# A hybrid attention/mLSTM layer on one core: low parts of the normalised input on GpSimd, their products one place later, two low parts of the weights ahead of sums, wider dummy products

## The chip, the core and the metric

The kernel runs on one NeuronCore of a Trainium2 chip. The metric is the device time of the program in microseconds (us), the median of several executions. Before the change it is 353.72 us (three runs, 353.4 to 353.92).

## The reference, cut to what matters

One layer, 256 tokens of width 1024, fp32. Only the first lines bear on this change:

```
ada = c @ w_ada + b_ada                                   # c: one row of 1024
shift, scale, gate = split(ada, 3)
h = rmsnorm(x, norm_w) * (1 + scale) + shift              # [256, 1024]
qa, ka, va, za, qm, km, vm, zm, om, ig, fg, ga, gm = split(h @ w_in)   # w_in: [1024, 11272]
...  # attention over qa, ka, va; a chunked mLSTM over qm, km, vm; two projections; gates
y = sigmoid(ga) * ya + sigmoid(gm) * ym
return x + gate * (y @ w_out)
```

## The kernel before

**Split products.** An fp32 matrix product is made of three passes of a faster type (fp32r). Each operand is written as a high part (the value rounded to fp32r) and a low part (the value less the high part), and high x high, high x low and low x high are added up in PSUM. For each piece of weights ScalarE makes the high part (`wrh`, later `wh`) by a cast, VectorE the low part (`wrl`, later `wl`) by a subtraction of two tiles. The normalised input gets the same: `hTh` and `hTl`, [128, 8, 256], with the 1024 rows of h in eight slices of 128.

**The norm phase** is the first 52 us. The eight slices k = 0..7 are worked off one after the other while their data stream in. For each, `adat` (two pieces of 512 KB: the columns of w_ada for scale and shift of that slice) and 128 rows of w_in (the first 1784 columns and the eight gate columns) are loaded on SyncE's queue in the order A0 W0 A1 W1 and so on. The sums over `adat` times c give the slice's scale `Ab` and shift `Bb`, ScalarE applies these to the transposed x, and TensorE adds the slice's products to four accumulators: `pm0`, `pm1`, `pm2` (512 columns each, two token halves) and `pg` (256). No scheduler is at work: each engine runs its instructions in the order in which they are written, and that order is the string `P1_STEPS`. A step is a letter and a slice number:

- `c`, `k`: VectorE's sums for scale and shift over `adat` (L152); `C` both for slice 0 (L145). `a`, `b`: ScalarE makes `Ab` (L156) and `Bb` (L160) of them
- `i`, `j`: ScalarE writes `hTh` (L166) and the unrounded `hf` (L170); `G`: the low part `hTl` = hf - hTh (L173); `H`: i and j of slice 0
- `w`, `x`, `y`: ScalarE's high parts of the weights, columns 0 to 512, 512 to 1024, 1024 to 1792 (L178). `U`, `z`, `v`: VectorE's low parts of the same three (L183)
- `P`, `Q`, `q`, `N`, `M`, `n`, `m`, `e`: products on TensorE (L194). A pair (ch, i) is accumulator ch and pass i, and one such pair is two matmuls, one for each token half. For accumulator 0 pass 1 is high x low of the weights and pass 2 the one with `hTl`; for the others pass 1 is the one with `hTl` and pass 2 that with the low weights
- `K`: dummy products on the identity, so that TensorE does not lie idle; `D`, `E`: transposes of x by a product with `diag`, for the first and second token half; `t`: copies of them; `R`: GpSimd fills a small table (L279, L284); `L`: next loads

Ahead of the steps stand `keep_clock(WARM)`, then four products `pc` that spread c over all partitions, ScalarE's copies of them to `cb` (the second operand of all sums), the sum of squares of x for the first token half on VectorE and for the second on ScalarE (L239), two small GpSimd steps that make `rsx` of each (L213, L214), and ScalarE's two `diag` tiles (L242), which scale the identity by rsx.

In the main phase after it (from 51.6 us) chunks of weights are split and multiplied in the same manner, without a step that the change touches.

Of the kernel before, what the change touches and what calls it, by code (L numbers as in the profile page):

```python
# [9 lines left out]
F32 = mybir.dt.float32  # L10
F32R = mybir.dt.float32r
AF = mybir.ActivationFunctionType
OP = mybir.AluOpType
# [25 lines left out]

P1_STEPS = ("K5 D0 D1 D2 E0 E1 E2 C0 w0 R0 R1 R2 R3 U0 H0 G0 t0 B0 P0 x0 z0 y0 t2 B1 t1 L1 c1 a1 w1 k1 v0 Q0 q0 n0 T3 m0 "
            + "".join(f"b{k} i{k} U{k} j{k} G{k} x{k} " + ("t3 " if k == 2 else "") + f"L2 c{k + 1} z{k} y{k} a{k + 1} "
                      f"w{k + 1} k{k + 1} v{k} e{k} " for k in range(1, 7))
            + "b7 i7 U7 j7 G7 x7 z7 y7 v7 P7 Q7 q7 N7 M7").split()
WARM = 5

KX = 248
NR = 1536 + KX + 8
# [15 lines left out]
def tile_hybrid(ctx: ExitStack, tc: tile.TileContext, x, c, params, params2, w_row, ada_mod, ada_gate,  # L65
                w_in, w_att_proj, w_ml_proj, w_out, out):
    nc = tc.nc
# [15 lines left out]
    ident = consts.tile([128, 128], F32, name="ident")  # L83
# [5 lines left out]
    hTh = consts.tile([128, KT, S], F32R, name="hTh")  # L89
    hTl = consts.tile([128, KT, S], F32R, name="hTl")  # L90
# [36 lines left out]
    adat, wrow, wsp, hf = {}, {}, {}, {}  # L127
# [21 lines left out]
    def modulation_sum(k, s):  # L149
        if s:  # L150
            sums[k] = ph.tile([128, 2], F32, name="sums", bufs=2)
        nc.vector.tensor_tensor_reduce(sq, adat[k][:, s], cb, 1.0, 0.0, OP.mult, OP.add, sums[k][:, s:s + 1])  # L152
# [9 lines left out]
    def modulate(k, parts="ij"):  # L162
        kc = slice(k, k + 1)
        src = xnT[:, k] if k else xps[0][:, 0]
        if "i" in parts:
            nc.scalar.activation(hTh[:, k], src, AF.Identity, scale=Ab[:, kc], bias=Bb[:, kc])  # L166
        if "j" not in parts:
            return
        hf[k] = ph.tile([128, S], F32, name="hf", bufs=2)
        nc.scalar.activation(hf[k], src, AF.Identity, scale=Ab[:, kc], bias=Bb[:, kc])  # L170

    def modulate_low(k):
        nc.vector.tensor_tensor(hTl[:, k], hf[k], hTh[:, k].bitcast(F32), op=OP.subtract)  # L173

    def split_hi(k, c0, c1, copy=nc.scalar.copy):
        if k not in wsp:
            wsp[k] = (ph.tile([128, NR], F32R, name="wrh", bufs=3), ph.tile([128, NR], F32R, name="wrl", bufs=3))
        copy(wsp[k][0][:, c0:c1], wrow[k][:, c0:c1])  # L178

    def split_low(k, e, c0, c1):  # L180
        h, l = wsp[k]
        cs = slice(c0, c1)
        e.tensor_tensor(l[:, cs], wrow[k][:, cs], h[:, cs].bitcast(F32), op=OP.subtract)  # L183

    def mm_row(k, ch, passes=(0, 1, 2)):
        h, l = wsp[k]
        n = 512 if ch < 3 else NR - 1536
        cs = slice(ch * 512, ch * 512 + n)
        ops = ((hTh, h), (hTl, h), (hTh, l)) if ch else ((hTh, h), (hTh, l), (hTl, h))
        for i in passes:  # L190
            a, b = ops[i]
            for t in range(2):

                nc.tensor.matmul(pm[ch][:, t], a[:, k, t * 128:(t + 1) * 128], b[:, cs],  # L194
                                 start=k == 0 and i == 0 and (ch < 3 or t == 0),
                                 stop=k == KT - 1 and i == 2 and (ch < 3 or t == 1), skip_group_check=ch == 3)
# [4 lines left out]
    def next_loads(n):  # L201
        while n and lp[0] < len(P1_LOADS):
            (load_ada if P1_LOADS[lp[0]][0] == "A" else load_row)(int(P1_LOADS[lp[0]][1]))
            lp[0] += 1
            n -= 1
# [15 lines left out]
    pw = pp.tile([128, 2, 512], F32, name="warm", tag="pm0")  # L221

    def keep_clock(n):
        for _ in range(n):
            nc.tensor.matmul(pw[:, 0, 0:128], ident, ident, start=True, stop=True)

    keep_clock(WARM)


    pc = [pp.tile([128, 512], F32, name="pc0", tag="pg"), pp.tile([128, D], F32, name="pc1", tag="pm2")]  # L230
    for j in range(4):
        n, q = divmod(j, 2)
        nc.tensor.matmul(pc[n][:, q * 256:(q + 1) * 256], pick[:, j:j + 1].to_broadcast([128, 128]), cparts,
                         start=q == 0, stop=q == 1, skip_group_check=True)
# [12 lines left out]
    def x_transposes(kp, ts=(0, 1)):  # L247
        if 0 in ts:
            xps[kp] = pp.tile([128, 2, 256], F32, name="xps", tag=("pm1", "aux1", "pg", "aux1")[kp])
        pa = xps[kp]  # L250
        for t in ts:
            for kk in range(2):
                k = 2 * kp + kk
                o, v = pa[:, kk, t * 128:(t + 1) * 128], xt[:, t, k * 128:(k + 1) * 128]
                nc.tensor.matmul(o, v, diag[:, t], start=t == 0 and kk == 0, stop=t == 1 and kk == 1,
                                 skip_group_check=True)
# [13 lines left out]
    def some(*what):  # L270
        return lambda k: [mm_row(k, ch, (i,)) for ch, i in what]
# [22 lines left out]

    for step in P1_STEPS:
        op, k = step[0], int(step[1])
        if op == "L":
            next_loads(k)
        else:
            dict(C=modulation, H=modulate, R=rel_prep, K=keep_clock, T=x_transposes, t=x_copy, B=open_banks,  # L300
                 D=lambda k: x_transposes(k, (0,)), E=lambda k: x_transposes(k, (1,)),
                 w=lambda k: split_hi(k, 0, 512), x=lambda k: split_hi(k, 512, 1024), y=lambda k: split_hi(k, 1024, NR),
                 U=lambda k: split_low(k, nc.vector, 0, 512), z=lambda k: split_low(k, nc.vector, 512, 1024),
                 v=lambda k: split_low(k, nc.vector, 1024, NR), G=modulate_low,
                 c=lambda k: modulation_sum(k, 1), k=lambda k: modulation_sum(k, 0),
                 a=modulation_scale, b=modulation_shift, i=lambda k: modulate(k, "i"), j=lambda k: modulate(k, "j"),
                 P=lambda k: mm_row(k, 0), Q=lambda k: mm_row(k, 1, (0, 1)), q=lambda k: mm_row(k, 1, (2,)),
                 N=lambda k: mm_row(k, 2), M=lambda k: mm_row(k, 3),
                 n=some((2, 0), (2, 1), (3, 0), (3, 1)), m=some((2, 2), (3, 2)),
                 e=some((0, 0), (0, 1), (0, 2), (1, 0), (1, 1), (1, 2), (2, 0), (2, 1), (3, 0), (3, 1), (2, 2), (3, 2))  # L310
                 )[op](k)


# [185 lines left out]
    f = slice(32, 36)  # L499
# [424 lines left out]
    for g in range(NG):  # L924
# [32 lines left out]
        for kk in range(2):  # L957
            k = 2 * kp + kk
            first, last = k == 0, k == KT - 1
            if ch["name"] == "out":  # L960

                for i in (0, 1):
                    for t, c0 in ((0, 0), (0, 256), (1, 0), (1, 256)):
                        a = (sh_, sl_)[i][:, k, t * 128:(t + 1) * 128]
                        cs = slice(c0, c0 + 256)
                        for w in (wh, wl)[:2 - i]:
                            nc.tensor.matmul(mmt[ci][:, t, cs], a, w[:, kk, cs],  # L967
                                             start=first and i == 0 and c0 == 0 and w is wh,
                                             stop=last and i == 1 and c0 > 0, skip_group_check=True)
            elif ch["kind"] == "tok":  # L970
                for t in range(2):
                    a, b = sh_[:, k, t * 128:(t + 1) * 128], sl_[:, k, t * 128:(t + 1) * 128]
# [14 lines left out]
    for t, c0, n in ((0, 0, 512), (1, 0, 256), (1, 256, 256)):  # L987
        pt = ps.tile([128, n], F32, name="mm", bufs=2)
        for k in range(KT):
            a, b = T["yh"][:, k, t * 128:(t + 1) * 128], T["yl"][:, k, t * 128:(t + 1) * 128]  # L990
# [54 lines left out]
```

## Time and profile before

| | us |
|---|---|
| median of 3 runs | 353.72 (353.4 to 353.92) |
| the profiled execution, its own time | 354.01 |
| its span, first to last instruction | 352.2 |
| TensorE busy | 345.3 (98%) |
| VectorE, ScalarE, GpSimd busy | 240.7, 209.9, 83.0 |

A profile row reads: start, length, engine, source line, operation, the tile written and the tiles read, how many instructions are merged in it, and in brackets the idle time of the engine just before and what ended it. PE is TensorE, DVE VectorE, ACT ScalarE, POOL GpSimd. The page's list of a group has its count, total and mean. "8.6 to 13.9" in a line's own view are the first and last start, and three numbers with strokes the shortest, median and longest duration in ns. A matmul of plain fp32 operands has two records. The records of matmuls overlap, so that on TensorE a row's length is longer than the distance to the next row. Lines of the program behind L225 have a number one higher in the changed kernel.

### The profile page before, as it was taken

Reading aid. Unit: us, or ns where it says so; the run is one execution under the profiler, and the core shown is the slowest. Engines: PE = TensorE matmul, PEld = TensorE weight load, DVE = VectorE, ACT = ScalarE, POOL = GpSimd, SP = SyncE. Lnnn points to the kernel's source line nnn. Section 1 sums busy time; section 2 is a strip of 40 time slices with the busy share of each in tenths; the row PEclk is TensorE's granted clock in tenths of the full one; section 3 lists DMA queues with packets and bytes.
Section 4 is the critical chain, followed back from the end, with each engine's and each line's share of the span. In section 5 each row is a group of like instructions: output and inputs, shape, how many; then the busy total and the mean of one; then the engine's idle time right before and its main releaser. Section 6 shows DMA issues by size and latency. Waiting matters only on the chain.

```text
span 352.2 us, 6126 instructions
## 1 busy us (share of the span) xinstructions
PE 345.3 (98%) x2424; PEld 321.0 (91%) x2424; DVE 240.7 (68%) x363; ACT 209.9 (60%) x328; POOL 83.0 (24%) x79
## 2 busy tenths in 40 slices
PE   7999999999999999999999999999999999999996
PEld 6778889888999999999999888888899999999995
DVE  5889988869974428767774474764475775469961
ACT  4867789996885766674654435545646374544510
POOL 4700006582006052555240000000010320452000
PEclk9999999999999999999999999999999999999999
DMA  8999999995680453493664955649219229382011
GB/s 299 418 417 419 412 384 337 237 261 217 220 308 13 139 220 125 147 370 137 239 241 131 378 207 214 265 151 379 66 26 359 95 60 358 123 271 88 2 61 60
DMA packets 25140, 77.98 MB, mean 221 GB/s; under 512 B 2960, under 2 KB 6040, under 8 KB 24600
## 3 DMA queue, kind: packets, MB, share of 16 engines
q1 hardware_dynamic: 24816, 77.03, 61.3%
q10 hardware_dynamic: 296, 0.56, 0.5%
q8 instruction: 19, 0.31, 0.4%
q14 instruction: 9, 0.07, 0.1%
HBM read 76.14 MB, written 1.45 MB: 220 GB/s over the span
## 4 chain that ended last, share of the span: by engine, by line
PE 92%; DMA 7%; DVE 0%; issue 0%; DVEq 0%
PE mm L984 15%; PE mm L981 15%; PE mm L983 15%; PE mm L974 9%; PE mm L975 9%; PE mm L976 9%; PE pm L194 6%; DMA adat<-in_ada_mod_dram 6%; PE mm L967 3%; PE aux L737 1%; PE pg L194 1%; PE mm L996 1%; PE aux L634 1%; PE mm L995 1%; PE mm L994 1%; DMA xt<-in_x_dram 1%
## 5 line engine op out<-in xcount | busy, mean ns | idle before, releaser
L444 DVE TENSOR_TENSOR wl<-raw,wh 128x1024 fp32r<-128x1024 f32 (+1 forms) x92 | 115.8, 1268 | 68.0 <-ACT wh L440 68.0
L440 ACT CAST wh<-raw 128x1024 fp32r<-128x1024 f32 (+1 forms) x100 | 102.2, 1031 | 58.8 <-PE mm L976 29.4
L981 PE MATMUL mm<-hTh,wh 128*128 128x256 f32 x320 | 90.1, 282 | 0.0
L983 PE MATMUL mm<-hTl,wh 128*128 128x256 f32 x320 | 88.7, 277 | 0.0
L984 PE MATMUL mm<-hTh,wl 128*128 128x256 f32 x320 | 88.7, 277 | 0.0
L981 PEld LDWEIGHTS mm<-hTh,wh 128*128 128x128 f32 x320 | 60.2, 188 | 0.1
L983 PEld LDWEIGHTS mm<-hTl,wh 128*128 128x128 f32 x320 | 60.2, 188 | 0.1
L984 PEld LDWEIGHTS mm<-hTh,wl 128*128 128x128 f32 x320 | 60.2, 188 | 0.0
L974 PE MATMUL mm<-wh,hTh 128*128 128x512 f32 (+1 forms) x144 | 55.0, 382 | 0.0
L976 PE MATMUL mm<-wh,hTl 128*128 128x512 f32 (+1 forms) x144 | 54.4, 378 | 0.0
L975 PE MATMUL mm<-wl,hTh 128*128 128x512 f32 (+1 forms) x144 | 54.3, 377 | 0.0
L976 PEld LDWEIGHTS mm<-wh,hTl 128*128 128x128 f32 x144 | 27.0, 188 | 5.1
L974 PEld LDWEIGHTS mm<-wh,hTh 128*128 128x128 f32 x144 | 27.0, 188 | 4.7
L975 PEld LDWEIGHTS mm<-wl,hTh 128*128 128x128 f32 x144 | 27.1, 188 | 4.6
L444 POOL TENSOR_TENSOR wl<-raw,wh 128x1024 fp32r<-128x1024 f32 x8 | 19.5, 2456 | 18.4 <-ACT wh L440 18.4
L774 POOL TENSOR_SCALAR f<-f 128x4 f32<-128x4 f32 x2 | 0.4, 198 | 86.9 <-DVE f L773 86.9
L183 DVE TENSOR_TENSOR wrl<-raw,wrh 128x512 fp32r<-128x512 f32 (+1 forms) x24 | 18.1, 781 | 0.5 <-ACT wrh L178 0.4
L981 PE MATMUL mm<-yah,wh 128*128 128x256 f32 x64 | 18.3, 286 | 0.0
L152 DVE CUSTOM_DVE_ANT_0 sq<-adat,cb 128x1024 f32<-128x1024 f32 x14 | 17.1, 1221 | 1.1 <-DMA adat<-in_ada_mod_dram 1.1
L984 PE MATMUL mm<-yah,wl 128*128 128x256 f32 x64 | 17.7, 277 | 0.0
L983 PE MATMUL mm<-yal,wh 128*128 128x256 f32 x64 | 17.7, 277 | 0.0
L981 PE MATMUL mm<-ymh,wh 128*128 128x256 f32 x64 | 17.7, 276 | 0.0
(218 smaller groups left out, 663.8 us busy)
## 6 DMA issues: line engine op xcount, KB each, us to landing
raw<-in_w_in_dram SPq DMA_DIRECT2D x36, 1024.0 KB, 4.9
adat<-in_ada_mod_dram SPq DMA_DIRECT2D x16, 512.0 KB, 9.3
raw<-in_w_row_dram SPq DMA_DIRECT2D x8, 640.0 KB, 9.4
raw<-in_ada_gate_dram SPq DMA_DIRECT2D x4, 1024.0 KB, 5.6
raw<-in_w_att_proj_dram SPq DMA_DIRECT2D x4, 1024.0 KB, 7.9
raw<-in_w_ml_proj_dram SPq DMA_DIRECT2D x4, 1024.0 KB, 5.5
raw<-in_w_out_dram SPq DMA_DIRECT2D x4, 1024.0 KB, 4.8
raw<-in_w_row_dram SPq DMA_DIRECT2D x8, 256.0 KB, 9.3
```

What stands on the lines that cost most here:

```text
L152: nc.vector.tensor_tensor_reduce(sq, adat[k][:, s], cb, 1.0, 0.0, OP.mult, OP.add, sums[k][:, s:s + 1])
L183: e.tensor_tensor(l[:, cs], wrow[k][:, cs], h[:, cs].bitcast(F32), op=OP.subtract)
L194: nc.tensor.matmul(pm[ch][:, t], a[:, k, t * 128:(t + 1) * 128], b[:, cs], start=k == 0 and i == 0 and (ch < 3 or t == 0), stop=k == KT - ...
L440: nc.scalar.copy(h, w)
L444: e.tensor_tensor(l, w, h.bitcast(F32), op=OP.subtract)
L967: nc.tensor.matmul(mmt[ci][:, t, cs], a, w[:, kk, cs], start=first and i == 0 and c0 == 0 and w is wh, stop=last and i == 1 and c0 > 0, sk ...
L974: nc.tensor.matmul(o, a, wh[:, kk], start=first, stop=False)
L975: nc.tensor.matmul(o, a, wl[:, kk], start=False, stop=False)
L976: nc.tensor.matmul(o, b, wh[:, kk], start=False, stop=last)
L981: nc.tensor.matmul(o, wh[:, kk, cs], sh_[:, k], start=first and i % 2 == 0, stop=False, skip_group_check=True)
L983: nc.tensor.matmul(o, wh[:, kk, cs], sl_[:, k], start=False, stop=False, skip_group_check=True)
L984: nc.tensor.matmul(o, wl[:, kk, cs], sh_[:, k], start=False, stop=last and i % 2 == 1, skip_group_check=True)
```

## The change

Four edits, all in the norm phase:

1. the low part `hTl` of slices 1 to 7 is made on GpSimd, that of slice 0 stays on VectorE;
2. in `e`, the products of slices 1 to 6, the first pair of accumulator 1 goes ahead of the pair of accumulator 0 that reads `hTl`; slice 7 uses `e` too, in place of its own order;
3. in slices 2 and 3, `z` (the low part of columns 512 to 1024) goes ahead of the sum `c` of the next slice;
4. the dummy products have 512 columns instead of 128, and there are three instead of five in each of the two groups.

```
-P1_STEPS = ("K5 D0 D1 D2 E0 E1 E2 C0 w0 ...
-            + "".join(f"b{k} i{k} U{k} j{k} G{k} x{k} " + ("t3 " if k == 2 else "") + f"L2 c{k + 1} z{k} y{k} a{k + 1} "
-                      f"w{k + 1} k{k + 1} v{k} e{k} " for k in range(1, 7))
-            + "b7 i7 U7 j7 G7 x7 z7 y7 v7 P7 Q7 q7 N7 M7").split()
-WARM = 5
+P1_STEPS = ("K3 D0 D1 D2 E0 E1 E2 C0 w0 ...
+            + "".join(f"b{k} i{k} U{k} j{k} G{k} x{k} " + ("t3 " if k == 2 else "") + f"L2 "
+                      + (f"z{k} c{k + 1} " if k in (2, 3) else f"c{k + 1} z{k} ") + f"y{k} a{k + 1} w{k + 1} k{k + 1} v{k} e{k} " for k in range(1, 7))
+            + "b7 i7 U7 j7 G7 x7 z7 y7 v7 e7").split()
+WARM = 3
...
     def modulate_low(k):
-        nc.vector.tensor_tensor(hTl[:, k], hf[k], hTh[:, k].bitcast(F32), op=OP.subtract)
+        (nc.gpsimd if k else nc.vector).tensor_tensor(hTl[:, k], hf[k], hTh[:, k].bitcast(F32), op=OP.subtract)
...
     def keep_clock(n):
         for _ in range(n):
-            nc.tensor.matmul(pw[:, 0, 0:128], ident, ident, start=True, stop=True)
+            nc.tensor.matmul(pw[:, 0].rearrange("p (r n) -> p r n", r=4), ident, ident[:, None, :].to_broadcast([128, 4, 128]),
+                             start=True, stop=True)
...
-                 e=some((0, 0), (0, 1), (0, 2), (1, 0), (1, 1), (1, 2), (2, 0), (2, 1), (3, 0), (3, 1), (2, 2), (3, 2))
+                 e=some((0, 0), (0, 1), (1, 0), (0, 2), (1, 1), (1, 2), (2, 0), (2, 1), (3, 0), (3, 1), (2, 2), (3, 2))
```

TensorE's list at the start, before; `pc` are the products that feed `cb`, `xps` the transposes of x.

```order
L225 MATMUL warm<-ident 128x128 x5
L233 MATMUL pc_131<-cparts,pick 128x256 x2
L233 MATMUL pc_132<-cparts,pick 128x256 x2
L225 MATMUL warm<-ident 128x128 x5
L255 MATMUL xps<-diag,xt 128x128 x12
```

And after:

```order
L225 MATMUL warm<-ident 128x512 x3
L234 MATMUL pc_129<-cparts,pick 128x256 x2
L234 MATMUL pc_130<-cparts,pick 128x256 x2
L225 MATMUL warm<-ident 128x512 x3
L256 MATMUL xps<-diag,xt 128x128 x12
```

The places are the same; ahead of `pc`, and again ahead of the transposes, stand 3 x 512 dummy columns where there were 5 x 128.

VectorE's list in slice 2, before, from U2 to U3. The lines L152 are the sums c3 and k3, each with the read of its accumulator.

```order
L183 TENSOR_TENSOR wrl<-raw,wrh 128x512
L173 TENSOR_TENSOR hTl<-hf,hTh 128x256
L152 ISA sq,sums<-adat,cb 128x1024
L152 ISA sums 128x1
L183 TENSOR_TENSOR wrl<-raw,wrh 128x512
L152 ISA sq,sums<-adat,cb 128x1024
L152 ISA sums 128x1
L183 TENSOR_TENSOR wrl<-raw,wrh 128x768
L183 TENSOR_TENSOR wrl<-raw,wrh 128x512
```

And after; the `x2` at its ends are U2 with z2, and U3 with z3:

```order
L183 TENSOR_TENSOR wrl<-raw,wrh 128x512 x2
L152 ISA sq,sums<-adat,cb 128x1024
L152 ISA sums 128x1
L152 ISA sq,sums<-adat,cb 128x1024
L152 ISA sums 128x1
L183 TENSOR_TENSOR wrl<-raw,wrh 128x768
L183 TENSOR_TENSOR wrl<-raw,wrh 128x512 x2
```

The low part hTl is gone from the list, z2 stands ahead of c3, and k3 follows c3 with nothing between.

GpSimd's list from the end of the table's filling to the main phase, after; before, L173 was not in it, and the rest was the same.

```order
L285 COPY rvec<-prm 8x14
L285 COPY rvec<-prm 8x143
L173 TENSOR_TENSOR hTl<-hf,hTh 128x256 x7
L504 MEMSET gt 128x128
L470 TENSOR_SCALAR ms<-ms 128x8
```

The seven low parts stand behind the filling of the table and ahead of the clearing of `gt`, which the main phase reads.

More of the change, by code (lines that the diff above doesn't have):

```diff
@@ L37 @@
 P1_LOADS = "A0 W0 A1 W1 A2 W2 A3 W3 A4 W4 A5 W5 A6 W6 A7 W7".split()
-P1_STEPS = ("K5 D0 D1 D2 E0 E1 E2 C0 w0 R0 R1 R2 R3 U0 H0 G0 t0 B0 P0 x0 z0 y0 t2 B1 t1 L1 c1 a1 w1 k1 v0 Q0 q0 n0 T3 m0 "
-            + "".join(f"b{k} i{k} U{k} j{k} G{k} x{k} " + ("t3 " if k == 2 else "") + f"L2 c{k + 1} z{k} y{k} a{k + 1} "
-                      f"w{k + 1} k{k + 1} v{k} e{k} " for k in range(1, 7))
-            + "b7 i7 U7 j7 G7 x7 z7 y7 v7 P7 Q7 q7 N7 M7").split()
-WARM = 5
+P1_STEPS = ("K3 D0 D1 D2 E0 E1 E2 C0 w0 R0 R1 R2 R3 U0 H0 G0 t0 B0 P0 x0 z0 y0 t2 B1 t1 L1 c1 a1 w1 k1 v0 Q0 q0 n0 T3 m0 "
+            + "".join(f"b{k} i{k} U{k} j{k} G{k} x{k} " + ("t3 " if k == 2 else "") + f"L2 "
+                      + (f"z{k} c{k + 1} " if k in (2, 3) else f"c{k + 1} z{k} ") + f"y{k} a{k + 1} w{k + 1} k{k + 1} v{k} e{k} " for k in range(1, 7))
+            + "b7 i7 U7 j7 G7 x7 z7 y7 v7 e7").split()
+WARM = 3
 KX = 248
```

## The prediction

> **What bounds the kernel now.** I read the chain first, then who TensorE waits for, then the first 35 us of each engine in time.
>
> ```profile
> span 352.2 us, 6126 instructions
> PE 92%; DMA 7%; DVE 0%; issue 0%; DVEq 0%
> ```
> ```profile
> PE warm L225 <- POOL ident masks.py:199: 1.4, 1, 1.4
> PE xps L255 <- ACT diag L242: 0.8, 1, 0.8
> PE pm L194 <- DVE wrl L183: 0.6, 1, 0.6
> PE pm L194 <- ACT hTh L166: 0.5, 1, 0.5
> ```
>
> The chain is TensorE's. The four waits are all that TensorE has in the whole span, and they lie in the first 25 us; after that it runs to the end without a gap. So what the change does to the moment at which TensorE leaves the row products (the norm phase) goes into the time one to one, and nothing behind it can give it back. TensorE in time (start, length, group):
>
> ```profile
> 1.35 2.50 PE L225 MATMUL warm<-ident 128*128 128x128 f32 x10 [1.35 <-POOL ident masks.py:199]
> 3.94 1.23 PE L233 MATMUL pc<-cparts,pick 128*128 128x256 f32 x4
> 4.96 1.48 PE L225 MATMUL warm<-ident 128*128 128x128 f32 x10
> 7.24 2.94 PE L255 MATMUL xps<-diag,xt 128*128 128x128 f32 x24 [0.79 <-ACT diag L242]
> 10.68 0.74 PE L194 MATMUL pm<-wrh,hTh 128*128 128x512 f32 x2 [0.50 <-ACT hTh L166]
> ...
> 16.83 0.63 PE L194 MATMUL pm<-wrh,hTh 128*128 128x512 f32 x2
> ...
> 23.48 0.61 PE L194 MATMUL pm<-wrh,hTl 128*128 128x512 f32 x2
> 24.74 0.73 PE L194 MATMUL pm<-wrl,hTh 128*128 128x512 f32 x2 [0.64 <-DVE wrl L183]
> ...
> 27.56 0.62 PE L194 MATMUL pm<-wrh,hTh 128*128 128x512 f32 x2
> ...
> 32.37 0.63 PE L194 MATMUL pm<-wrh,hTh 128*128 128x512 f32 x2
> ```
>
> Slice 0 begins at 10.68, slice 1 at 16.83, slice 3 at 27.56; a slice without waits is 32.37 - 27.56 = 4.81 us, nine pairs of 512 columns and three of 256, so 0.46 a pair. Slice 2 holds the wait for the low part z2 (24.74 instead of about 23.94). VectorE shows why z2 is late:
>
> ```profile
> 7.28 1.34 DVE L145 CUSTOM_DVE_ANT_0 sq<-adat,cb,b 128x1024 f32<-128x1024 f32 x1 [1.29 <-ACT diag L242]
> ...
> 8.67 1.28 DVE L145 CUSTOM_DVE_ANT_0 sq<-adat,cb,prm 128x1024 f32<-128x1024 f32 x1
> ...
> 16.50 0.43 DVE L173 TENSOR_TENSOR hTl<-hf,hTh 128x256 fp32r<-128x256 f32 x1
> ...
> 22.85 1.22 DVE L152 CUSTOM_DVE_ANT_0 sq<-adat,cb 128x1024 f32<-128x1024 f32 x1 [1.11 <-DMA adat<-in_ada_mod_dram]
> ...
> 24.00 0.69 DVE L183 TENSOR_TENSOR wrl<-raw,wrh 128x512 fp32r<-128x512 f32 x1
> ...
> 27.66 1.22 DVE L152 CUSTOM_DVE_ANT_0 sq<-adat,cb 128x1024 f32<-128x1024 f32 x1
> ...
> 28.81 0.69 DVE L183 TENSOR_TENSOR wrl<-raw,wrh 128x512 fp32r<-128x512 f32 x1
> 29.41 1.22 DVE L152 CUSTOM_DVE_ANT_0 sq<-adat,cb 128x1024 f32<-128x1024 f32 x1
> ...
> 30.55 1.56 DVE L183 TENSOR_TENSOR wrl<-raw,wrh 128x768 fp32r<-128x768 f32 x2
> 32.13 0.42 DVE L173 TENSOR_TENSOR hTl<-hf,hTh 128x256 fp32r<-128x256 f32 x1
> ```
>
> It stands behind the sum c3, which waits for its load until 22.85. From 27.66 on VectorE is as full as TensorE: c 1.15 (27.66 to 28.81), z 0.60, k 1.14, v and U 1.58, G 0.34 (32.13 to the next c at 32.47) make 4.81.
>
> **The dummies.** Ten records are five matmuls. One record of the first group takes 0.42, so the pace is (2.50 - 0.42)/9 = 0.23 us a record, 0.21 without the start; in the second (1.48 - 0.28)/9 = 0.13. TensorE at its full pace:
>
> ```profile
> L225 PE MATMUL warm<-ident x20: 275/418/579, 1.4 to 6.2; 128*128 128x128 f32 x20
> ```
> ```profile
> 159.74 1.31 PE aux L737 x8
> ```
>
> L737 is two fp32 products of 128 and two of 256 columns, 12 times 128 with both records counted: 0.11 per 128, and time goes with columns. So the second group holds about two slow records and then fast ones: the pace doubles near 5.4. Now there are six records of 512 columns ahead of pc, 0.87 us each at the slow pace and 0.44 at the fast: from 1.35 to 5.4 some 4.7 of them, the other 1.3 in 0.6 us. TensorE comes to pc at 6.0, not 3.94. What is queued behind is not idle matter: pc feeds cb, and ScalarE's list goes on behind cb.
>
> ```profile
> 4.78 1.07 ACT L236 COPY cb<-pc 128x512 f32<-128x512 f32 x2 [1.78 <-PE pc L233]
> 5.74 1.07 ACT L239 ACTIVATE xnT<-xt 128x1024 f32<-128x1024 f32 x1
> ...
> 7.89 0.40 ACT L242 ACTIVATE diag<-ident,rsx 128x128 f32<-128x128 f32 x1 [0.70 <-POOL rsx L214]
> ...
> 10.06 0.56 ACT L166 ACTIVATE hTh<-xps,Bb,Ab 128x256 fp32r<-128x256 f32 x1 [0.43 <-DVE Bb L145]
> ```
> ```profile
> 6.98 0.22 POOL L213 TENSOR_SCALAR rsx<-ssx 128x1 f32<-128x1 f32 x1 [0.31 <-ACT xnT L239]
> 7.29 0.57 POOL L214 TENSOR_TENSOR rsx<-rsx,mhalf 128x1 f32<-128x1 f32 x1
> 7.81 0.87 POOL L279 COPY rvec<-prm 8x16 f32<-8x16 f32 x1
> ```
> ```profile
> L284 POOL COPY rvec<-prm x16: 175/183/1295, 8.6 to 13.9; 8x3 f32<-8x3 f32 x3, 8x4 f32<-8x4 f32 x2, 8x6 f32<-8x6 f32 x2, 8x10 f32<-8x10 f32 x2
> ```
>
> The copies of cb start 0.45 behind pc at the fast pace (0.84 at the slow), so 6.45, and end at 7.5 instead of 5.85. VectorE's first sum starts at 7.55 instead of 7.28 and the second ends at 10.2 instead of 9.95: that alone would cost 0.3. The square of x starts at 7.4 instead of 5.74, and GpSimd's two steps on rsx, which began 1.24 behind it, at 8.65 instead of 6.98. There they meet VectorE's long sums, which they now just miss. GpSimd does not get through while VectorE runs such an operation: the copy at 7.81 ends at 8.68, right after VectorE's 7.28 + 1.34 = 8.62, and tiny copies whose median is 0.18 take up to 1.3. So the 0.22 step waits out the first sum (8.9), the 0.57 step, asked for at 9.0, the second one, and ends 0.4 behind it, at 10.65. The second diag moves from 7.89 to 10.7 and ends at 11.1; then come the transposes of the second token half, twelve records at 0.11, to 12.45, where hTh has its first four at 11.75 (10.06 before). Slice 0 begins at 12.5, 1.8 late. Bounds: 0 if all of it were hidden, and the 2.6 that follow if the pace stays slow (below).
>
> **Low parts of h on GpSimd.** Seven pieces of 0.34 us leave VectorE's list. What comes for them no row of GpSimd shows at 128x256; the nearest:
>
> ```profile
> 76.26 0.72 POOL L526 TENSOR_TENSOR G<-G 4x256 f32<-4x256 f32 x1
> ```
> ```profile
> 109.02 1.29 POOL L642 TENSOR_TENSOR yal<-yf,yah 128x512 fp32r<-128x512 f32 x1 [22.02 <-ACT yah L641]
> ```
> ```profile
> 109.92 1.47 DVE L444 TENSOR_TENSOR wl<-raw,wh 128x1024 fp32r<-128x1024 f32 x1 [1.63 <-ACT wh L440]
> ...
> 114.26 1.23 DVE L444 TENSOR_TENSOR wl<-raw,wh 128x1024 fp32r<-128x1024 f32 x1 [2.27 <-ACT wh L440]
> ```
>
> 256 columns take 0.72, and partitions do not count. The last two rows are the point: VectorE's subtraction, 1.23 alone, takes 1.47 when it meets GpSimd's, and ends at 111.39, 1.08 behind GpSimd's end at 110.31: it did not run beside it, it waited, only its 0.15 of start was hidden. All of VectorE's work in this phase reads two tiles as that one does. So each low part takes 0.72 - 0.15 = 0.57 out of VectorE's time, where it took 0.34 before. It also waits: the step takes its turn behind the operation that VectorE is in, up to 1.1 us. Bounds: nothing, if these operations did run together, and 0.72 plus a whole sum. I take 0.57, the row's own behaviour.
>
> VectorE's slice: 1.15 + 0.60 + 1.14 + 0.87 (v) + 0.60 (U) = 4.36 (0.11 of the 1.58 was G waiting for hf); with 0.57 it is 4.93, against TensorE's 4.81. VectorE becomes the bound of slices 3 to 6. In slices 2 and 3 c is followed by k at once, and k waits for c's result (8.67 is 0.05 behind the end at 8.62, where 28.81 is 0.07 ahead of one): 0.12 more.
>
> **The order.** The product with hTl one place later gives 0.46 us of room; it needs it, since the low part now ends later. z2 ahead of c3 takes the wait of slice 2 away: slices 1 and 2 took 27.56 - 16.83 = 10.73, 1.1 more than twice 4.81, and up to that comes back. z3 ahead of c4 gains nothing, as c4 did not wait. The last slice issues its same twelve products in the order of the others, so that the first bank is whole one place later; the copies out of it lie beside the products that follow, so nothing, and 0.46 if TensorE wanted that bank at once. The SP list is unchanged; its loads wait for tiles that VectorE frees later by what TensorE is late too.
>
> **The sum**, by slices. Start: +1.8, slice 1 at 18.6. Slice 1: hf, taken at 16.50 before, is ready at 18.3, when c2 has just begun; the low part runs 19.3 to 19.9, TensorE asks for it at 18.6 + 3 x 0.46 = 20.0 with 0.1 of passing on: a wait of 0.2, and 0.1 for the first matmul behind a wait (24.74's 0.73 against 0.62): +0.3, slice 2 at 23.7. VectorE comes to c3 at 24.6, when the load has long landed, so no DMA wait is left; v2 comes 0.1 late: +0.2, -1.1 for what is gone: slice 3 at 28.7, 1.15 behind 27.56. Slices 3 to 6: VectorE 5.05 + 3 x 4.93 = 19.84 against 19.24, +0.6, and three restarts of 0.1: +0.9. Together 1.8 + 0.3 + 0.2 - 1.1 + 0.9 = +2.1. The profiled execution took 354.01 (span 352.2), 0.3 above the median 353.72; on it that is 356.1, on the median 355.8.
>
> **Rivals.** (1) Faster: only z2 counts. If GpSimd and VectorE ran together and the start were hidden, slice 2's wait goes and nothing takes its place: 0.8 of it to be had, 352.9. For it: the 0.64 wait is real and c3 behind it had a load to wait for. Against: rows 109.92 and L284. It decides if slice 0 starts before 11.0. (2) The low parts cost, the dummies not: were TensorE at full pace much earlier, cb at 5.9, the start stays; slice 2 then gives back 0.5 (z2 in time, v2 behind the low part not), and slices 3 to 6 take 0.9: 354.1. Against it: the first group's 0.21 a record. (3) The dummies cost, the low parts not: the late start of 0.9 (no wait at rsx) is swallowed by the 1.1 of waits that go, with 0.1 left: 353.6, the same as before. Against: the 1.47. (4) The pace doubles later. The six records then end at 1.35 + 6 x 0.87 = 6.6, pc takes 0.9, cb is there at 8.3 instead of 7.5: 0.8 more, 356.6. Before, a late doubling cost nothing, since the transposes waited for ScalarE anyway.
>
> The Trainium skill, "TensorE: Matmul & The Clock Gate", Part 1, says the clock is released after a busy window of about 3.4 us that runs freely, so that the moment varies with where the first matmul falls in it. The 4.05 us from 1.35 to 5.4 agree with it; by that rule rival 4 is not an accident but a share of the executions, and its time is the 356.6 above. The page's advice to warm up for 4 us or more speaks for the wider dummies; the row at 4.96 shows that the narrower ones had got there.
>
> **Chances.** The sum 0.60 (its own range 355.2 to 356.4), rival 4 0.12, rival 2 0.11, rival 3 0.09, rival 1 0.08. A measurement of this kernel tells about 0.2%, 0.7 us, from no change. Faster is rival 1: 0.07. The same: rivals 2 and 3 and the rest of 1, less what of 2 lies above 354.4: 0.19. Slower: 0.74. The range takes the sum, rivals 4 and 2: 354.0 to 356.7, leaving out rivals 1 and 3.
>
> **What would show it.** In the profile after: pc near 6.0; the second diag at about 10.7 and waiting for POOL rsx; slice 0 at 12.5; no DVE wait for adat near 22; hTl rows on POOL of 0.72 to 1.8, and sums behind them of about 1.7 instead of 1.22; TensorE waits of 0.1 to 0.3 for POOL hTl and DVE wrl between 20 and 48. I am wrong if pc starts before 5, if the steps on rsx slip in between the two sums (then the start is 0.9 late), or if sums keep 1.22 beside hTl rows.

## Result and the profile after

The changed kernel takes 356.26 us (median of 5 runs, 355.69 to 357.04) against 353.72 for the one before (5 runs, 353.4 to 354.05): a ratio of 1.0073, 95% interval 1.0056 to 1.009, slower by 2.5 us. A second set of six runs gave 1.008 (1.0067 to 1.0094). The profiled execution took 355.69 with a span of 353.9, one of the two fastest of the five; that of before took 354.01 with a span of 352.2, the slower end of its runs. The traces differ by 1.7 us, and the rest of the 2.5 lies between executions.

The change: its span and its chain from the page, and all waits of TensorE.

```profile
span 353.9 us, 6110 instructions
PE 90%; DMA 7%; DVE 1%; issue 1%; SPq 0%; DVEq 0%
...
PE warm L225 <- POOL ident masks.py:199: 1.4, 1, 1.4
PE xps L256 <- ACT diag L243: 0.6, 1, 0.6
PE pm L194 <- DVE wrl L183: 0.2, 1, 0.2
```

The waits named are fewer than before (0.8 us behind the dummies' own start, where there were 1.9), and the kernel is slower: what TensorE lost at the start is mostly dummy work, and the small stops between slices are too short to be listed. They are read from where the slices start. TensorE in time, after; the later rows are the first products of slices 0, 1, 2, 3 and 7:

```profile
1.35 4.41 PE L225 MATMUL warm<-ident 128*128 128x512 f32 x6 [1.35 <-POOL ident masks.py:199]
5.20 1.03 PE L234 MATMUL pc<-cparts,pick 128*128 128x256 f32 x4
6.07 2.74 PE L225 MATMUL warm<-ident 128*128 128x512 f32 x6
8.64 1.50 PE L256 MATMUL xps<-diag,xt 128*128 128x128 f32 x12
10.73 1.60 PE L256 MATMUL xps<-diag,xt 128*128 128x128 f32 x12 [0.59 <-ACT diag L243]
12.10 0.72 PE L194 MATMUL pm<-wrh,hTh 128*128 128x512 f32 x2
...
18.15 0.64 PE L194 MATMUL pm<-wrh,hTh 128*128 128x512 f32 x2
...
23.25 0.62 PE L194 MATMUL pm<-wrh,hTh 128*128 128x512 f32 x2
...
28.29 0.62 PE L194 MATMUL pm<-wrh,hTh 128*128 128x512 f32 x2
...
48.41 0.63 PE L194 MATMUL pm<-wrh,hTh 128*128 128x512 f32 x2
```

Of before, two starts that the prediction did not need, slices 2 and 7:

```profile
21.66 0.62 PE L194 MATMUL pm<-wrh,hTh 128*128 128x512 f32 x2
...
46.82 0.62 PE L194 MATMUL pm<-wrh,hTh 128*128 128x512 f32 x2
```

Slice 7 starts 1.59 later, and from there to the end the two traces are alike to within 0.08. Each trace also records when TensorE's granted clock comes up to full, which is when its pace doubles: at 5.38 before and at 4.54 in the change. The start of the after-trace on ScalarE, VectorE and GpSimd:

```profile
6.03 1.07 ACT L237 COPY cb<-pc 128x512 f32<-128x512 f32 x2 [3.03 <-PE pc L234]
10.28 0.40 ACT L243 ACTIVATE diag<-ident,rsx 128x128 f32<-128x128 f32 x1 [1.84 <-POOL rsx L214]
```
```profile
7.14 1.34 DVE L145 CUSTOM_DVE_ANT_0 sq<-adat,cb,b 128x1024 f32<-128x1024 f32 x1 [1.21 <-ACT cb L237]
8.53 1.28 DVE L145 CUSTOM_DVE_ANT_0 sq<-adat,cb,prm 128x1024 f32<-128x1024 f32 x1
```
```profile
8.24 0.33 POOL L213 TENSOR_SCALAR rsx<-ssx 128x1 f32<-128x1 f32 x1 [1.60 <-ACT xnT L240]
8.65 1.59 POOL L214 TENSOR_TENSOR rsx<-rsx,mhalf 128x1 f32<-128x1 f32 x1
```

The L214 step, 0.57 before, is asked for while VectorE is in its first sum and ends at 10.24, behind the second (8.53 + 1.28 = 9.81). The second diag and half of the transposes stand behind it. In the slices, GpSimd's low parts and what VectorE does around them:

```profile
17.95 1.67 POOL L173 TENSOR_TENSOR hTl<-hf,hTh 128x256 fp32r<-128x256 f32 x1 [4.70 <-ACT hf L170]
22.85 0.74 POOL L173 TENSOR_TENSOR hTl<-hf,hTh 128x256 fp32r<-128x256 f32 x1 [3.23 <-ACT hf L170]
```
```profile
17.81 1.22 DVE L152 CUSTOM_DVE_ANT_0 sq<-adat,cb 128x1024 f32<-128x1024 f32 x1
18.95 1.22 DVE L183 TENSOR_TENSOR wrl<-raw,wrh 128x512 fp32r<-128x512 f32 x1
...
23.32 0.82 DVE L183 TENSOR_TENSOR wrl<-raw,wrh 128x512 fp32r<-128x512 f32 x1 [0.53 <-ACT wrh L178]
...
28.56 0.82 DVE L183 TENSOR_TENSOR wrl<-raw,wrh 128x512 fp32r<-128x512 f32 x1 [0.53 <-ACT wrh L178]
```

Where the sum runs first, GpSimd's step waits and takes 1.67 instead of 0.74, and the low part of w_in behind the sum takes 1.22 instead of 0.69. Where z stands first (23.32, 28.56), VectorE idles 0.53 for ScalarE's copy.

### The profile page after: what moved, and what is told of

The parts are those of the page before. It is cut to its first block, busy times and chain, and to the rows that moved or that the text cites. A ratio compares the mean times of both kernels' runs of the same rounds, so it can differ in the third digit from the quotient of the medians.

```text
span 353.9 us, 6110 instructions
## 1 busy us (share of the span) xinstructions
PE 348.3 (98%) x2416; PEld 319.7 (90%) x2416; DVE 242.0 (68%) x356; ACT 210.0 (59%) x328; POOL 88.6 (25%) x86
## 4 chain that ended last, share of the span: by engine, by line
PE 90%; DMA 7%; DVE 1%; issue 1%; SPq 0%; DVEq 0%
PE mm L982 15%; PE mm L984 14%; PE mm L985 14%; PE mm L975 9%; PE mm L977 9%; PE mm L976 9%; DMA adat<-in_ada_mod_dram 7%; PE pm L194 5%; PE mm L968 3%; PE aux L738 1%; PE aux L635 1%; PE mm L996 1%; PE mm L997 1%; PE mm L995 1%; PE aux L485 1%; PE aux L597 1%
## 5 line engine op out<-in xcount | busy, mean ns | idle before, releaser
L183 DVE TENSOR_TENSOR wrl<-raw,wrh 128x512 fp32r<-128x512 f32 (+1 forms) x24 | 20.5, 880 | 3.3 <-ACT wrh L178 3.3
L984 PE MATMUL mm<-yml,wh 128*128 128x256 f32 x64 | 17.7, 276 | 0.0
```

The lines of the kernel that those rows point to most:

```text
L984: nc.tensor.matmul(o, wh[:, kk, cs], sl_[:, k], start=False, stop=False, skip_group_check=True)
```

## The experiments

Three parts of the change can be had apart: W the wide dummies, G the low parts on GpSimd, Z the moved z2 and z3. The later place of the product with hTl goes with G or Z, except in the runs that say otherwise. Ratios are to before on the same chip, where before took 353.4 to 353.7.

| run | parts | median us | ratio (95%) | first sum | slice 0 | slices 1 to 6 over 28.86 |
|---|---|---|---|---|---|---|
| before, profiled | none | 353.72 | 1 | 7.28 | 10.68 | 1.13 |
| the change | W G Z | 356.26 | 1.0073 (1.0056 to 1.009) | 7.14 | 12.10 | 1.40 |
| e12 | W G Z | 356.58 | 1.008 (1.0067 to 1.0094) | 7.19 | 12.15 | 1.44 |
| e1 | G Z | 354.49 | 1.0032 (1.002 to 1.0044) | 7.22 | 10.62 | 1.60 |
| e2 | W | 354.39 | 1.0034 (1.0022 to 1.0046) | 8.30 | 13.26 | 0.00 |
| e3 | W Z | 355.56 | 1.0058 (1.0046 to 1.007) | 7.95 | 12.91 | 0.57 |
| e4 | z2 alone, old place | 353.43 | 1.0004 (0.9995 to 1.0012) | 7.36 | 10.76 | 0.52 |
| e5 | W G | 356.08 | 1.0066 (1.0052 to 1.008) | 7.97 | 12.93 | 0.69 |
| e6 | G | 354.54 | 1.0025 (1.0014 to 1.0037) | 8.06 | 11.46 | 0.93 |
| e7 | W G Z, square first | 355.87 | 1.0062 (1.0048 to 1.0075) | 7.82 | 11.67 | 1.42 |
| e8 | W, but one ahead of pc | 354.03 | 1.0013 (1.0002 to 1.0023) | 7.95 | 11.35 | 0.05 |
| e9 | G twice, Z | 358.27 | 1.0135 (1.0116 to 1.0153) | 7.13 | 10.75 | 5.25 |
| e10 | G Z, old place | 354.89 | 1.004 (1.0027 to 1.0054) | 7.05 | 10.45 | 1.98 |
| e11 | Z | 353.54 | 1.0003 (0.999 to 1.0015) | 6.88 | 10.28 | 0.94 |

The last three columns are of the profiled execution: the start of VectorE's first L145 sum, of slice 0's first product on TensorE, and (start of slice 7 less start of slice 1) less six times 4.81.

**e1, the change with narrow dummies.**

```
-K3 ... WARM = 3, 512 columns
+K5 ... WARM = 5, 128 columns
```

> The change with the dummies of before (five of 128 columns ahead of pc and five behind it), the rest of the change kept: GpSimd's low parts, their products one place later, two low parts of w_in ahead of sums. My theory (the wide dummies stand ahead of pc in TensorE's list, pc feeds cb, and the start slips; the low parts cost a second, smaller share): pc starts at 3.9 again, slice 0 at 10.7, and what is left is the pace of slices 1 to 6, +0.5 us on before's 353.7: 354.2, with runs as close together as those of before (0.7 us), since the moment at which TensorE's pace doubles no longer passes into the start. Rival (the dummies are hidden, all of the loss is GpSimd's low parts): slice 0 may move, but the time stays at 356.3. Second rival (the low parts cost nothing, as the dummies took it all): 353.0, by the wait for z2 that goes.

```profile
3.51 1.15 PE L233 MATMUL pc<-cparts,pick 128*128 128x256 f32 x4
...
10.62 0.73 PE L194 MATMUL pm<-wrh,hTh 128*128 128x512 f32 x2 [0.83 <-ACT hTh L166]
```

Slice 0 is back at 10.62, and over half of the loss is gone: the dummies are not hidden. What is left, 0.32%, is more than the 0.5 us that I expected (0.7 to 1.6 us by the interval). Runs spread over 0.9 us.

**e2, the wide dummies alone.**

```
+K3 ... WARM = 3, 512 columns     (before otherwise)
```

> Before with the wide dummies alone (three of 512 columns ahead of pc and three behind it). My theory: pc starts at 5.2 to 6.6 instead of 3.94, by the moment at which the pace doubles, which differs between executions; slice 0 starts 1.4 to 2.3 later; the waits of slices 1 and 2 (0.6 for wrl, about 0.5 behind hTh) swallow a part of that, so the time is 0.4 us above before when the pace doubles at 4.45, 0.7 when it doubles at 5.4 and 1.5 when it does at 7 or later: 354.1 to 355.2, and a spread of the runs of 1 us or more. Rival (the dummies are hidden): 353.7 and the spread of before. Second rival (the whole late start passes on, nothing is swallowed): 355.2 to 356.

```profile
1.35 5.49 PE L225 MATMUL warm<-ident 128*128 128x512 f32 x6 [1.35 <-POOL ident masks.py:199]
5.85 1.54 PE L234 MATMUL pc<-cparts,pick 128*128 128x256 f32 x4
...
13.26 0.73 PE L194 MATMUL pm<-wrh,hTh 128*128 128x512 f32 x2
```
```profile
8.30 1.35 DVE L145 CUSTOM_DVE_ANT_0 sq<-adat,cb,b 128x1024 f32<-128x1024 f32 x1 [2.29 <-ACT cb L237]
```
```profile
9.81 1.59 POOL L214 TENSOR_TENSOR rsx<-rsx,mhalf 128x1 f32<-128x1 f32 x1
```

As expected: 0.34%, 1.2 us, and a spread of 1.3 us. In this execution (the slowest of its five) the six records take 5.49, none of them at the fast pace: the trace's record of the clock has the pace double at 6.89, 2.35 us later than in the change's trace. Slice 0 starts 2.58 later than before, and slices 1 to 6 take exactly 6 x 4.81: started this late, VectorE never waits for a load, and 1.13 of the late start is swallowed.

**e3, the change with all low parts on VectorE.**

```
-        (nc.gpsimd if k else nc.vector).tensor_tensor(hTl[:, k], ...
+        nc.vector.tensor_tensor(hTl[:, k], ...
```

> The change with all low parts of h on VectorE again, the rest kept (wide dummies, products one place later, z2 and z3 ahead of sums). My theory: the start is as late as in the change (1.4 to 2.3), and slices 1 to 6 gain what GpSimd's low parts cost there, 0.8 us: 354.8 to 355.8, 0.8 under the change in the median, with its wide spread. Rival (the low parts on GpSimd cost nothing): the same time as the change, 356.3. Second rival (all of the loss is theirs): 353.7 or less.

```profile
7.95 1.34 DVE L145 CUSTOM_DVE_ANT_0 sq<-adat,cb,b 128x1024 f32<-128x1024 f32 x1 [1.46 <-DMA adat<-in_ada_mod_dram]
```

In range, but it tells more beside e2, which has the same dummies and no moved steps: with them slices 1 to 6 take 0.57 more, all of it in slices 2 and 3. So the moved z2 and z3, for which I had booked a gain, cost something in these traces. The row shows the second thing: here it is the load, landing late, that holds the first sum.

**e4, z2 alone.**

```
+ f"z{k} c{k + 1} " if k == 2 else f"c{k + 1} z{k} "     (before otherwise)
```

> Before with one step moved: the low part z2 of w_in's row block 2 ahead of the sum c3 that waits for its load; nothing else. My theory: TensorE's wait of 0.64 for wrl in slice 2 goes, but VectorE then comes to c3 no sooner than its load lands and the steps behind it, k3 and v2, end 0.3 later, so half of it comes back: 353.4, 0.3 faster. Rival (the wait comes back in full at v2, since VectorE is as full as TensorE from there on): 353.7. Second rival (all of the wait is gained): 353.1.

```profile
27.13 1.23 DVE L152 CUSTOM_DVE_ANT_0 sq<-adat,cb 128x1024 f32<-128x1024 f32 x1 [0.23 <-DMA adat<-in_ada_mod_dram]
```

No difference (0.05% less to 0.12% more): the rival by which it all comes back. Half of the wait, which I expected to gain, would have been a ratio of 0.9992, outside the interval. The trace shows where a part of it goes: slice 2 is shorter (5.03, where the profile of before has 5.90), but now the next sum, c4, comes early enough to wait for its load, and slice 3 takes 5.11 instead of 4.81.

**e5, the change without the moved z2 and z3.**

```
-(f"z{k} c{k + 1} " if k in (2, 3) else f"c{k + 1} z{k} ")
+f"c{k + 1} z{k} "
```

> The change with z2 and z3 behind the sums c3 and c4 again, as before; wide dummies, GpSimd's low parts and the later products kept. The theory after the first four runs: the moved steps cost. With z first, VectorE waits 0.53 for ScalarE's copy of the block (two rows of the change), which c covered, and 0.12 for the result of c ahead of k; its cycle in slices 2 and 3 is 5.24 in the change's trace instead of 4.92 (34.32 to 39.23, where c is first). So both back: 2 x 0.3 = 0.6 under the change, 355.4 on the chip where before takes 353.4, a ratio of 1.0055, and no idle row of VectorE for the copy. Rival, the prediction's own term: the moves gain up to 1.1 where a load is late and nothing else; then this run is the same as the change (1.0073) when no load is late, or slower.

```profile
28.44 1.21 DVE L152 CUSTOM_DVE_ANT_0 sq<-adat,cb 128x1024 f32<-128x1024 f32 x1
...
33.34 1.21 DVE L152 CUSTOM_DVE_ANT_0 sq<-adat,cb 128x1024 f32<-128x1024 f32 x1
```

The trace says yes: no idle time for the copy, a cycle of 33.34 - 28.44 = 4.90, and slices 1 to 6 are 0.71 shorter than in the change. The time says it less clearly, 1.0066 with an interval that takes in the change's 1.0073: the gain of 0.6 us is seen in the one trace and not established in the medians.

**e6, the low parts on GpSimd alone** (with the later product).

```
+        (nc.gpsimd if k else nc.vector).tensor_tensor(hTl[:, k], ...     (before otherwise)
```

> Before with the low parts of h on GpSimd (all but the first) and their products one place later, nothing else: narrow dummies, z2 and z3 behind the sums. Theory: slice 0 at 10.6 to 10.7; slice 1 loses 0.2; slice 2 has the wait for the sum's load that before has; slices 3 to 6 lose 0.11 each, VectorE's cycle being 4.92 against TensorE's 4.81: together 0.6 over before, 354.0 (1.0018), under the 354.5 of the run that has the moved steps too. Rival (GpSimd's low parts run beside VectorE and cost nothing): 353.4. Second rival (the low parts are all of what the run with narrow dummies lost, the moved steps nothing): 354.5 (1.0032).

```profile
5.00 2.34 PE L225 MATMUL warm<-ident 128*128 128x128 f32 x10
```

0.25%, 0.9 us, between the theory's 0.6 and the second rival's 1.1, and both ends lie in the interval; the first rival (no cost) is out. Its slices 2 to 6 take 4.92, 4.95, 4.88, 4.91 and 4.88.

**e7, the change with the square ahead of cb.**

```
+    nc.scalar.activation(xnT[:, 4:8]..., xt[:, 1], AF.Square, ...); rstd(1)
     for n in range(2):
         nc.scalar.copy(cb[:, n * 512:(n + 1) * 512], pc[n][:, 0:512])
```

> The change with ScalarE's square of x ahead of the two copies of cb instead of behind them, nothing else. Theory: the second diag is late because the square stands behind pc and cb, and GpSimd's two steps on rsx then meet VectorE's sums. With the square first, it runs while TensorE is in the dummies, the L214 step takes 0.57 again instead of 1.59, the second diag starts at 7.3 to 8.3 instead of 10.28, and slice 0 starts about 0.9 behind the end of the second sum: 10.7 where pc starts at 5.2, 11.8 where it starts at 5.85. That is 1.4 earlier than in the change at the same pc. Slices 1 to 6 then are those of the run with narrow dummies, so the time is 354.5 to 355.0 (ratio 1.0032 to 1.0045), with the spread that the wide dummies give. Rival (the start is late because of pc alone, through cb and the sums): slice 0 moves by less than 0.3 at the same pc and the time stays at 1.0073.

```profile
7.22 0.57 POOL L214 TENSOR_TENSOR rsx<-rsx,mhalf 128x1 f32<-128x1 f32 x1
```
```profile
5.63 1.03 PE L234 MATMUL pc<-cparts,pick 128*128 128x256 f32 x4
6.49 2.74 PE L225 MATMUL warm<-ident 128*128 128x512 f32 x6
9.07 2.84 PE L256 MATMUL xps<-diag,xt 128*128 128x128 f32 x24
11.67 0.72 PE L194 MATMUL pm<-wrh,hTh 128*128 128x512 f32 x2
```

The mechanism is as said: the step takes 0.57 again and both halves of x go through in one group of 24. With the square behind cb, slice 0 would have started 4.96 behind a first sum that waits for cb, as in every other run with three wide dummies ahead of pc (below); here it is 3.85 behind it. The time is another matter: 1.0062 instead of the 1.0032 to 1.0045 that I gave, with an interval that takes in the change's 1.0073, so that the gain stands in the trace and is not established in the medians. Two things were left out: the square waits for x until 5.68 and pushes cb back, to 6.73 (e5, with pc at 5.66, has it at 6.50), and the dummies behind pc run to 9.07, so that TensorE comes to the transposes late itself.

**e8, one wide dummy ahead of pc, three behind.**

```
+K3 ... WARM = 1, 512 columns     (before otherwise)
```

> Before with the wide dummies, but one ahead of pc instead of three, and three behind it. Theory: only what stands ahead of pc counts. Two records of 0.87 to 1.0 at the slow pace end at 3.2; pc at 3.3, cb ends by 5.2, ahead of the load of the first sum, so slice 0 starts at 10.6 to 10.8 as before; the three behind pc (2.7 to 5.2 long) end at 8 to 9 at the latest. The time is that of before, 353.4 (0.999 to 1.002), and the spread too. Rival (the dummies behind pc hold up the first transposes as well, when the pace doubles late): 353.8 to 354.2 with a spread of 1 us.

```profile
1.35 2.07 PE L225 MATMUL warm<-ident 128*128 128x512 f32 x2 [1.35 <-POOL ident masks.py:199]
3.94 1.23 PE L234 MATMUL pc<-cparts,pick 128*128 128x256 f32 x4 [0.51 <-DVE cparts L124]
4.96 3.82 PE L225 MATMUL warm<-ident 128*128 128x512 f32 x6
8.62 2.84 PE L256 MATMUL xps<-diag,xt 128*128 128x128 f32 x24
11.35 0.74 PE L194 MATMUL pm<-wrh,hTh 128*128 128x512 f32 x2
```

Three quarters of a microsecond of e2's 1.2 are gone (the difference is uncertain by nearly 0.6 us): pc waits for its own operand again, and slice 0 stands 3.40 behind the first sum, which waits for its load till 7.95. What remains, 0.13%, has an interval that begins just above nothing; its median of 354.03 is where the rival put it, and its runs spread over 1.2 us. The trace speaks for the rival too: the first diag is there at 7.2, but TensorE comes to the transposes only at 8.62, behind the dummies. In e7 the 24 of them, with nothing to wait for, take 2.60 to the first product of slice 0 (9.07 to 11.67), so here slice 0 could not have started before 11.22. The late load hides this; with a load as early as in before, where slice 0 starts at 10.68, it would cost some 0.5 us, as an estimate from these rows.

**e9, each of GpSimd's low parts twice**, narrow dummies.

```
+        for _ in range(2 if k else 1):
             (nc.gpsimd if k else nc.vector).tensor_tensor(hTl[:, k], ...
```

> The run with narrow dummies (ratio 1.0032, 354.5 where before takes 353.4), with each of GpSimd's low parts of h issued twice, so that the suspected cost is doubled; the second one writes the same values again. Theory (GpSimd's step and VectorE's operations on two tiles exclude each other): every further step takes 0.57 out of VectorE's time in each slice from 1 to 6, the cycle goes from 4.92 to about 5.5, and the time to 357.5 to 358 (1.0115 to 1.013). Rival (they run side by side; the second step only makes hTl 0.74 later): the later product has 0.46 of room, so at most 0.3 a slice: 354.5 to 356.3 (up to 1.008), and VectorE's rows keep 1.22 and 0.69.

```profile
PE pm L195 <- POOL hTl L174: 3.1, 5, 1.1
```
```profile
22.12 1.89 POOL L174 TENSOR_TENSOR hTl<-hf,hTh 128x256 fp32r<-128x256 f32 x2 [2.62 <-ACT hf L170]
```
```profile
23.33 1.76 DVE L152 CUSTOM_DVE_ANT_0 sq<-adat,cb 128x1024 f32<-128x1024 f32 x1
...
33.53 1.22 DVE L152 CUSTOM_DVE_ANT_0 sq<-adat,cb 128x1024 f32<-128x1024 f32 x1
34.67 1.22 DVE L184 TENSOR_TENSOR wrl<-raw,wrh 128x512 fp32r<-128x512 f32 x1
35.82 1.74 DVE L152 CUSTOM_DVE_ANT_0 sq<-adat,cb 128x1024 f32<-128x1024 f32 x1
...
38.97 1.21 DVE L152 CUSTOM_DVE_ANT_0 sq<-adat,cb 128x1024 f32<-128x1024 f32 x1
```

1.0135, a touch above the theory's range and far from the rival's 1.008. In this kernel lines behind L173 have a number one higher. With two steps on GpSimd both the subtraction (1.22 for 0.69) and the sum behind it (1.74 for 1.21) lose 0.53, and VectorE's cycle is 38.97 - 33.53 = 5.44, against 4.91 with one (the change; the expectation of e5 names its two starts): 0.53 for each step. TensorE now waits for hTl as well, which adds to it.

**e10, the product with hTl in its old place**, narrow dummies.

```
-e=some((0, 0), (0, 1), (1, 0), (0, 2), (1, 1), ...
+e=some((0, 0), (0, 1), (0, 2), (1, 0), (1, 1), ...
```

> The run with narrow dummies (1.0032), with the product of hTl in its old place, so that TensorE asks for hTl one pair (0.46) sooner, and the last slice's rows in that order too. Theory: in slice 1 hTl is ready at about 17.2 to 18.3 and asked for at 18.1 instead of 18.6, a wait of at most 0.4; in slices 2 to 6 the step starts as soon as hf is there and VectorE is the one that is late: 0.2 to 0.5 over the run with narrow dummies (1.0038 to 1.0046). Rival (the low part comes late in every slice and the later place hides it): 0.46 in each of six slices, 357.2 (1.011).

```profile
PE pm L194 <- POOL hTl L173: 0.4, 1, 0.4
```

One wait of 0.4, in one slice, and 1.004 against e1's 1.0032: within the theory's range, and not the 0.46 in each slice. The later place is worth some 0.4 us between these two traces (1.98 and 1.60 in the table); the 0.3 us between the medians is less than their uncertainty.

**e11, the moved z2 and z3 alone** (with the later product), and **e12, the change once more.**

```
e11: +(f"z{k} c{k + 1} " if k in (2, 3) else f"c{k + 1} z{k} ")     +e=some((0, 0), (0, 1), (1, 0), (0, 2), ...     (before otherwise)
```

> Before with the moved steps alone: z2 and z3 ahead of c3 and c4 and the products of hTl one place later; narrow dummies, all low parts on VectorE. Theory: where a load of ada is late, the moves fill the wait of VectorE; where it is not, they cost 0.57 in slices 2 and 3 together (the trace with wide dummies and the same moves, against the one with wide dummies alone). With the start at 10.7 the loads are what VectorE waits for in either order, so the time is that of before: ratio 0.999 to 1.001. Rival (the moves cost their 0.57 here too): 1.0016. Second rival, the prediction's term of up to 1.1 gained: 0.997.

```profile
22.45 1.23 DVE L152 CUSTOM_DVE_ANT_0 sq<-adat,cb 128x1024 f32<-128x1024 f32 x1 [0.35 <-DMA adat<-in_ada_mod_dram]
```

No difference, 1.0003: with the early start the load is what VectorE waits for in either order.

> The change itself once more, for a second profile of it and for its runs beside others on one chip. Theory: the pace doubles at another moment (between 4.4 and 7 in the profiles so far) and the first load of ada lands at another one (6.9 to 7.9), so pc and slice 0 move together: slice 0 between 12.1 and 13.3, slice 1 to the end of the row products 1.4 over TensorE's own pace as in the first profile, and TensorE leaves the row products that much later; runs from 355.5 to 357, ratio 1.006 to 1.009. Rival (the start is always the 12.1 of the first profile, and the spread of the runs comes from a later place): slice 0 at 12.0 to 12.2 and the difference behind slice 1.

The second profile caught almost the same execution (the pace doubles at 4.63, pc starts at 5.25, slice 0 at 12.15), again the fastest of its runs, which go from 355.78 to 357.06. So it does not decide between theory and rival. That the slower executions start later is seen in the relatives of the change alone (e2, e3, e5: slice 0 at 12.91 to 13.26 with the same dummies), not in the change itself.

**What the runs give together.** Each part with and without the others, in per cent: W 0.34 alone, 0.41 on top of G (e5 less e6), 0.55 on Z (e3 less e11), 0.41 to 0.48 on both; G 0.25 alone, 0.29 on Z, 0.32 on W, 0.15 to 0.22 on both; Z 0.03 alone, 0.07 on G, 0.24 on W, 0.07 to 0.14 on both. Each difference is uncertain by nearly 0.2. The dummies are some 1.5 us, the low parts some 0.9, and the moved steps between nothing and 0.85, never a gain in the medians. No version was faster than the one before; the closest, e4 and e11, are the same as it.

**The start, in one rule of the table.** Slice 0 less first sum is 3.40 in before, e1, e4, e6, e8, e10 and e11, and 4.96 in the change, e2, e3, e5 and e12. The difference, 1.56, has two causes that overlap. The wide dummies behind pc keep TensorE from the transposes until 8.64 in the change, and with the 2.60 that 24 transposes take in e7, slice 0 could not have started before 11.24, 4.10 behind the first sum. The L214 step behind VectorE's second sum adds the other 0.86, which is about what e7 gets back (by the rule its slice 0 would have started at 12.57, with cb at 6.50 as in e5; it started at 11.67). No run has wide dummies ahead of pc and narrow ones behind it, so these two shares are worked out and not measured apart. The two others lie between, each with one of the causes: e9 (3.62, its second diag a microsecond later) and e7 (3.85, the transposes behind dummies). The first sum itself starts when cb and its load are both there, between 6.88 and 8.30 in these traces.

## Why the prediction was right, and where its steps were off

The forecast was 355.8 (354.0 to 356.7), slower; measured were 356.26 and, the second time, 356.58. By its own steps, in the profiled execution:

| step | predicted | measured |
|---|---|---|
| slice 0 starts | +1.8 (12.5) | 12.10 - 10.68 = +1.42 |
| slice 0 | 0 | 6.05 - 6.15 = -0.10 |
| slice 1 | +0.3 | 5.10 - 4.83 = +0.27 |
| slice 2 | -0.9 (-1.1 and 0.2) | 5.04 - 5.90 = -0.86 |
| slices 3 to 6 | +0.9 | 20.12 - 19.26 = +0.86 |
| sum | +2.1 | +1.59 |

The spans differ by 1.67; the 0.08 left over lies behind the start of slice 7, and every run with the last slice's new order has it (305.5 from there to the end, instead of 305.4). The signs and the places of the loss are right. That slice 2 and slices 3 to 6 agree so closely is luck, since their parts do not, as the items below show.

- **The start: mechanism right, pace mis-sized.** I had the pace double near 5.4, as in before; in this execution it doubles at 4.54, and cb comes at 6.03 instead of 6.45. In e5, which has the same dummies and the pace doubling at 5.48, it comes at 6.50, as the sum has it. The row of pc was misjudged by more (5.20 instead of 6.0), but cb follows it by 0.83 and not by 0.45, so that most of this cancels. From cb on all goes as the prediction has it: the square behind cb, the L214 step blocked by the second sum, the second diag right behind it. The distance from the first sum to slice 0, 7.55 to 12.5 in the prediction, is 4.95; measured are 4.96 in five profiles. What I did not price is the second group of dummies: without the late L214 step they alone would have held slice 0 back to 11.24, by the estimate above.
- **Rival 4 looks like the ordinary spread and not like a rival.** In the traces the pace doubles between 4.29 (e11) and 7.44 (e6, where all ten records of the second group are slow). The Trainium skill, "TensorE: Matmul & The Clock Gate", Part 1, has the moment vary by some 0.5 us either way, with where the first matmul falls in a window of about 3.4 us. The traces agree that it varies, and by more. With narrow dummies it does not reach the start: e6 and e10 (7.03) still have slice 0 3.40 behind the first sum. With three wide ones it stands ahead of pc, and e2 (6.89) starts slice 0 at 13.26. Against the profiled execution (355.69) the sum, 356.1, is 0.4 too high, and against the median it is 0.5 too low. That a later doubling makes the slower runs of the change is likely and not traced, since both of its profiles caught an early one. A late first load (the first sum at 7.95 to 7.97 in e3, e5 and e8) is the second cause of a late start, which I had not priced at all; kernels with narrow dummies have it too (e6, 8.06).
- **The gain of 1.1 in slice 2 was booked to the wrong part, and against the wrong execution.** The wait for the load did go, but by the late start: e2, with the old order, has no wait either. In the medians the moved z2 is worth nothing (e4, e11), and "z3 ahead of c4 gains nothing" should have been a cost: with z first VectorE idles 0.53 for ScalarE's copy, which c covered (in the change; where hTl is still on VectorE, as in e11, it fills most of that time). I had taken z's wait for c as the only one, and did not ask whether its copy was there. Also, the profiled execution of before was one of its slowest (354.01, where its medians are 353.4 to 353.7), so part of the 1.13 that it lost in slices 1 to 6 is likely to be missing in the usual one; that was not traced.
- **Slices 3 to 6: the sum right, the parts not.** 4.93 for VectorE's cycle is borne out (4.90 to 4.92), and 0.57 for a step is 0.53 in e9; GpSimd's own 0.72, read from a row of 4 partitions, is 0.74 at 128. But the change loses 0.43 and 0.29 in slices 3 and 4, where without the moved steps (e5) 0.06 and 0.10 are lost, and only 0.10 and 0.06 in 5 and 6; I had 0.12 in each and 0.4 of other costs.
- **Sums of 1.7 behind hTl rows**: not in the change. VectorE was nearly always in the sum already, GpSimd waited, and the subtraction behind it paid: 18.95 1.22 instead of 0.69. Where GpSimd came first the sum did pay, as in e9 (23.33 1.76). Either way it is 0.53. I had named sums that keep 1.22 as a sign of being wrong; they do keep it, and yet the price is there, one operation later.
- **The other rivals.** "Only z2 counts" and "the dummies not" fall with e1 and e2, "the low parts not" with e6 and e9.

The Trainium skill, "SBUF — State Buffer", section "Who interferes with whom", says that a VectorE instruction with two SBUF inputs and a GpSimd instruction that reads SBUF shut each other out for a whole instruction, and that the one that comes first decides who is blocked. The rows at 17.95 (GpSimd's step waits out a sum that came first) and 23.33 (a sum waits out GpSimd's step, in e9) show one case each.

## What to carry to other kernels

Filler on an in-order engine belongs behind the work that others wait for: three wide dummies ahead of one small product, and three more ahead of the transposes, moved a chain over four engines by 1.4 to 2.6 us, and made the start depend on when the clock comes up. Before a subtraction is moved to GpSimd, see whether VectorE's neighbours read two tiles; if so it costs VectorE more there (0.53) than at home (0.34). And a wait that one trace shows must be held against the spread of the runs before its removal is booked as a gain: a step may be moved out of one engine's shadow into another's.

## What was not expected of the hardware

The moment at which TensorE's pace doubles differed by 3.1 us between executions of like kernels (4.29 in e11, 7.44 in e6, with the first matmul always at 1.35). The first 512 KB load of ada held the first sum back to between 7.95 and 8.06 in four of the traces (e3, e5, e6, e8), while it let the sum start at 6.88 to 7.36 in the six others with narrow dummies; the order of the loads is the same in all. Three of these four profiles (e5, e6, e8) are from one chip and the fourth is not, so whether the chip has to do with it stays open. Beside that the start is rigid: the same distance of 3.40 or 4.96 from first sum to slice 0, to 0.01 us, over twelve profiles.
